# Two early weight loads on ScalarE's queue, one high part on VectorE, and the gate's small loads on SyncE's queue

## The chip, the cores and the metric

The kernel runs on one core of a Trainium2 chip. The metric is device time in microseconds (us); the time of a kernel is the median of its runs. The engines are named as in the profile: PE is TensorE (PEld its weight loads), DVE is VectorE, ACT is ScalarE, POOL is GpSimd, SP is SyncE. DMA issues can stand in the queue of SP, ACT or POOL.

## The reference

Two layers of an encoder trunk, in fp32, on x of 256 tokens by 2048 features. Each layer projects x once into many parts, runs three mixers side by side, multiplies each result by a SiLU gate, projects the concatenation back and normalizes:

```python
h = x @ w_in                                   # 2048 -> 6672 columns, cut into eleven parts
y_a = chunk_band_attention(a_q, a_k, a_v, rel_table)        # 8 heads of 128
log_g = log_sigmoid(b_lr @ gate_w + gate_b) / 16
y_b = rms(gla_chunk_recurrence(b_q, b_k, b_v, log_g)) * gla_norm_g   # 4 heads
mk, mv = split(mem @ w_mem_kv)                 # 256 memory tokens, 2048 -> 2 x 512
y_m = memory_attention(m_q, mk, mv)            # 4 heads of 128
y = concat([y_a * silu(a_z), y_b * silu(b_z), y_m * silu(m_z)])
x = layer_norm(alpha * x + y @ w_out)
```

## The kernel before

**Arithmetic.** PE multiplies in a rounded 32-bit form (fp32r). To keep fp32 accuracy each operand is split into a high part, the value rounded to fp32r, and a low part, the remainder. `parts` (L114) makes both: ACT casts the high part (L116), DVE subtracts it from the source for the low part (L117). A product is then three matmuls: high by high, low by high, high by low (`as_products`, L264, with x stationary and the weights moving; `ws_half`, L240, and `keys_of` with the weights stationary and the two parts of x side by side as the moving operand).

**Weights.** A piece of weights is two 128-row blocks of 512 columns (or four of 256, or two of 388). `piece` (L128) issues its load on SP into one of four `raw` buffers and splits it into one of four `wh` and one of four `wl` buffers. SP can issue a load once DVE has read the buffer's former contents, ACT can cast once PE is done with the former `wh`; so the loads, casts and subtractions run some pieces ahead of PE.

**Order.** PE's and SP's instructions keep the order in which the code writes them; DVE and ACT do so only inside the marked blocks, and elsewhere a scheduler places them. POOL's order is the scheduler's too. Waits between engines are semaphores. Behind the kernel's start the order is:

- six matmuls on a tile of zeros (L753), which PE runs as twelve passes, while the first data are on their way;
- `first_memory` (L191): the values and keys of the memory, in eight steps p of two 128-row blocks each. `first_pieces` (L153) issues and splits the loads of a step. In steps 0 and 1, for each of two blocks k: a 128 KB quarter of the memory's transpose (`x_part`, L163, into `early`, which lies in the tile `res`), the value weights (L177), the key weights (L179). The value weights of step 0, block 0 are cut in two halves of 256 columns, so that PE can start on the first half. All of these loads stand in SP's queue; DVE and ACT follow the written order here;
- `values_of` (L198) and `keys_of` (L205) are the products. In step 0, block 0 the values take twelve matmuls of 256 columns: the first half of the columns for both blocks of 128 tokens, then the second half;
- the query and key group of the gated linear attention (L783), then `gla_inputs` (L296): the gate matrix three times into `gwraw`, the gate bias `gb` and the norm's scale `ng`, five small loads on POOL's queue. ACT's copy at L305 and DVE's subtraction at L306 make the gate matrix's parts; they are used in `gla`, after the next group. In layer 0 the identity and a mask follow on SP (L789, L791);
- the value projections (L797), the attention heads, the gates, the output projection and the norm. In layer 1 the same without `first_memory`, and the norm at the end is split up by columns.

Of the kernel before, what the change touches and what calls it, by code (L numbers as in the profile page):

```python
# [8 lines left out]
F32 = mybir.dt.float32  # L9
# [4 lines left out]
ALU = mybir.AluOpType  # L14
# [4 lines left out]
P = 128  # L19
# [17 lines left out]
def hybrid_trunk_kernel(  # L37
# [7 lines left out]
    pe, dve, act, pool, sp = nc.tensor, nc.vector, nc.scalar, nc.gpsimd, nc.sync  # L45
# [42 lines left out]
    def nm(s):  # L88
        uid[0] += 1
        return f"{s}_{uid[0]}"  # L90

    def mm(o, l, r, start, stop):
        pe.matmul(o, l, r, start=start, stop=stop, skip_group_check=True)  # L93

    def bank():
        return psa.tile([P, 512], F32, name=nm("bk"), tag="bk")

    def scratch(shape, dtype=F32):
        return sc.tile(shape, dtype, name=nm("sc"), tag="sc")

    def small(shape, tag, bufs=1):
        return sm.tile(shape, F32, name=nm(tag), tag=tag, bufs=bufs)
# [6 lines left out]
    def operand():  # L109

        x = opp.tile([P, 4, 2, T], F32R, name=nm("x"), tag="x")
        return x[:, :, 0], x[:, :, 1], x.rearrange("p j h t -> p j (h t)")

    def parts(hi, lo, src):  # L114

        act.copy(hi, src)  # L116
        dve.tensor_tensor(lo, src, hi.bitcast(F32), op=ALU.subtract)  # L117
# [35 lines left out]
    def first_pieces(p, x):  # L153


        xsrc, j0 = memT[p // 2], p % 2 * 2
        xraw = early[:, p // 2]
        vsrc = w512[0, G_MV, p].rearrange("p (k n) -> p k n", k=2)
        ksrc = w512[0, G_MK, p // 2:8:4, :, j0 * 256:j0 * 256 + 512].rearrange("h p (k n) -> p k h n", k=2)
        raws, his, los = ([wp.tile([P, 2, 512], dt, name=nm(n), tag=n) for _ in range(2)]  # L160
                          for n, dt in (("raw", F32), ("wh", F32R), ("wl", F32R)))

        def x_part(j):  # L163
            sp.dma_start(xraw[:, j], xsrc[:, j])
            parts(x[0][:, j], x[1][:, j], xraw[:, j])

        def split(i, at):
            parts(his[i][at], los[i][at], raws[i][at])

        if p < 2:  # L170
            with tc.manual_schedule(engines={DVE, mybir.EngineType.Activation}):
                for k in range(2):
                    x_part(slice(j0 + k, j0 + k + 1))
                    cut = 2 if p == k == 0 else 1
                    for h in range(cut):
                        cs = slice(h * 512 // cut, (h + 1) * 512 // cut)
                        sp.dma_start(raws[0][:, k, cs], vsrc[:, k, cs])  # L177
                        split(0, (slice(None), k, cs))
                    sp.dma_start(raws[1][:, k].rearrange("p (h n) -> p h n", h=2), ksrc[:, k])  # L179
                    split(1, (slice(None), k))  # L180
        else:
            with tc.high_priority(AHEAD):
                x_part(slice(j0, j0 + 2))
                sp.dma_start(raws[0], vsrc)
                split(0, slice(None))
                for h in range(2):
                    sp.dma_start(raws[1][:, :, h * 256:(h + 1) * 256], ksrc[:, :, h])
                split(1, slice(None))
        return list(zip(his, los))

    def first_memory(mk, mv, each):  # L191

        memq = []
        accv = psd.tile([P, 2, 512], F32, name=nm("acc"), tag="acc")
        acck = psd.tile([P, 2, 2, T], F32, name=nm("acc"), tag="acc")
        blocks = [acck[:, b] for b in range(2)] + [bank().rearrange("p (h t) -> p h t", h=2) for _ in range(2)]

        def values_of(p, w, kk):  # L198

            for h in range(2 if p == kk == 0 else 1):  # L200
                cs = slice(h * 256, h * 256 + 256) if p == kk == 0 else slice(0, 512)
                for t in range(2):
                    as_products(accv[:, t, cs], t, memq, [x[:, :, cs] for x in w], p * 2 + kk, kk, -1 if h else 0)

        def keys_of(p, w, kk):  # L205
            (wh, wl), (xh, _, both), j = w, memq[p // 2], p % 2 * 2 + kk
            for b in range(4):
                mm(blocks[b].rearrange("p h t -> p (h t)"), wh[:, kk, b * P:(b + 1) * P], both[:, j], p == kk == 0, False)
            for b in range(4):
                mm(blocks[b][:, 1], wl[:, kk, b * P:(b + 1) * P], xh[:, j], False, p * 2 + kk == 15)  # L210

        late = None
        for p in range(8):
            if p % 2 == 0:
                memq.append(operand())
            v, k = first_pieces(p, memq[-1])
            for kk in range(2):
                values_of(p, v, kk)
                if p < 2:
                    keys_of(p, k, kk)  # L220
            if p == 6:
                late = k
            elif p > 1:
                if p == 7:
                    parts(*mv, accv)
                    for kk in range(2):
                        keys_of(6, late, kk)
                for kk in range(2):
                    keys_of(p, k, kk)
            each(p)  # L230
        for half in range(2):
            tmp = scratch([P, 2, T])
            if half == 0:
                total(tmp, acck[:, :, 0], acck[:, :, 1])
            else:
                for b in range(2):
                    total(tmp[:, b], blocks[2 + b][:, 0], blocks[2 + b][:, 1])
            parts(mk[0][:, half * 2:half * 2 + 2], mk[1][:, half * 2:half * 2 + 2], tmp)
# [21 lines left out]
    def total(dst, a, b, scale=1.0):  # L260
        act.mul(dst, b, scale)
        dve.scalar_tensor_tensor(dst, a, scale, dst, op0=ALU.mult, op1=ALU.add)  # L262

    def as_products(o, t, xq, w, kt, kk, first=0):  # L264
        wh, wl = w
        xh, xl, _ = xq[kt // 4]
        j, ts = kt % 4, slice(t * P, (t + 1) * P)
        mm(o, xh[:, j, ts], wh[:, kk], kt == first, False)
        mm(o, xl[:, j, ts], wh[:, kk], False, False)
        mm(o, xh[:, j, ts], wl[:, kk], False, kt == 15)  # L270
# [25 lines left out]
    def gla_inputs(l):  # L296

        gw = sm.tile([P, 256], F32R, name=nm("gw"), tag="gw")
        raw = hd.tile([48, 256], F32, name=nm("gwraw"), tag="pairs0")
        gb = small([P, 2], "gb")  # L300
        ng = small([P, 1], "ng")
        for i in range(3):
            pool.dma_start(raw[i * 16:i * 16 + 16], gate_w[l])
        pool.memset(gw.bitcast(F32), 0.0)
        tc.keep_in_program_order(act.copy(gw[:48], raw))  # L305
        tc.keep_in_program_order(dve.tensor_tensor(gw[32:48], raw[32:], gw[32:48].bitcast(F32), op=ALU.subtract))  # L306
        pool.dma_start(gb, gate_b[l])
        pool.dma_start(ng, norm_g[l])
        return gw, gb, ng

    def gla(gw, gb, ng, gq, gk, lr, asv, yraw):
# [438 lines left out]
    zeros = hd.tile([P, P], F32, name="zeros", tag="st")  # L750
    dve.memset(zeros, 0.0)
    idle = bank()
    for _ in range(6):  # L753
        mm(idle[:, :P], zeros, zeros, True, True)

    res = per.tile([P, 2, D], F32, name="res")
# [3 lines left out]
    for l in range(L):  # L760
# [3 lines left out]
        if l == 0:  # L764
            def each(p):
                if p in (2, 4, 6, 7):
                    xq.append(resident_quarter(len(xq), xT[len(xq)]))

            first_memory(mk, mv, each)
        else:  # L770
            memq = []
# [13 lines left out]
        if l > 0:  # L785
            waiting.append(gens[1])
        gp = gla_inputs(l)
        if l == 0:
            sp.dma_start(ident, ident_d)  # L789
# [11 lines left out]
        def heads(g):  # L801
            t = hd.tile([P, 4, T], F32, name=nm("qk"), tag="qk", bufs=4)
            for i, a, b in ws_group(w512[l, g], xq):
                total(t[:, i:i + 2], a, b)
            return t
# [25 lines left out]
        for half in range(2):  # L831
            values(2 + half)
            q = heads(G_AQ0 if half == 0 else G_AQ1)
            k = heads(G_AK0 if half == 0 else G_AK1)
# [36 lines left out]
        gb = []  # L871
        rows = norm_rows(l) if last else None
        for n in range(WO_N):
            if last:
                g, b = scratch([P, 512]), scratch([P, 512])
            else:
                both = per.tile([P, 2, 512], F32, name=nm("gb"), tag=f"yr{n}")
                g, b = both[:, 0], both[:, 1]
# [126 lines left out]
```

## Time and profile before

| | |
|---|---|
| median of 3 runs | 925.89 us (925.69 to 926.02) |
| profiled execution, its own time | 925.59 us |
| span of the profile | 923.8 us |
| mean DMA rate over the span | 194 GB/s |
| DMA rate in the first two of 40 slices | 306 and 334 GB/s |
| software DMA queue (POOL's) | 1920 packets, 4.36 MB |

The rows are read like this. In a table by stretches, each row gives a stretch in us from the span's start, its length, the busy time of each engine with its count of instructions, the granted clock, the mean busy share of the DMA engines and their rate. In a timeline, a row gives the start, the time from the first to the end of the last of the merged instructions, the engine, the line, the operation, what it writes and reads, its shape and count, and in brackets how long the engine sat idle before it and what released it. A q behind an engine's name marks its queue (issues of DMAs, semaphores). In a row of a group by line and shape, the busy time and the mean ns stand behind the bar. In a row of one line, three durations in ns (least, median, greatest) and the first and last start stand behind the count; in a row of DMA issues, the size and the us from issue to landing.

### The profile page before, as it was taken

What the parts mean: (1) busy time and instruction counts of PE and PEld (TensorE: products, weight loads), DVE (VectorE), ACT (ScalarE), POOL (GpSimd) and SP (SyncE); (2) the same over time, 40 slices, a digit from 0 to 9 for tenths busy, and PEclk for the clock granted to TensorE, in tenths of its full rate; (3) what the DMA queues carried; (4) which work ended last, traced back from release to release, by engine and by line L of the source; (5) the groups of instructions that cost most, each with busy time, mean ns of one, the idle gap of its engine ahead of it and who ended that gap; (6) DMA issues with size and microseconds to landing.
All of it is one profiled execution on the core that took longest, in us unless ns stands there. A gap on an engine that the chain in (4) does not pass through costs nothing.

```text
span 923.8 us, 14249 instructions
## 1 busy us (share of the span) xinstructions
PE 916.7 (99%) x5500; PEld 806.5 (87%) x5500; DVE 587.9 (64%) x812; ACT 498.2 (54%) x714; POOL 21.8 (2%) x49
## 2 busy tenths in 40 slices
PE   9999999999999999999999999999999999999997
PEld 7889998998888888888888899889888888888885
DVE  6764478665564666555587666975655555766566
ACT  6644485484454675433566445754744555754350
POOL 1000000000000000000000000000000000110000
PEclk9999999999999999999999999999999999999999
DMA  9955865546554566756675466546555544667652
GB/s 306 334 189 174 306 207 173 161 165 194 183 162 160 171 206 200 219 193 196 227 249 164 150 205 204 193 154 196 170 193 166 164 152 160 199 222 223 198 163 92
DMA packets 71253, 178.85 MB, mean 194 GB/s; under 512 B 7304, under 2 KB 31240, under 8 KB 70928
## 3 DMA queue, kind: packets, MB, share of 16 engines
q1 hardware_dynamic: 69120, 173.30, 57.1%
q0 software_dynamic: 1920, 4.36, 1.8%
q8 instruction: 43, 0.70, 0.3%
q10 hardware_dynamic: 144, 0.26, 0.1%
q14 instruction: 26, 0.21, 0.1%
HBM read 175.77 MB, written 2.10 MB: 193 GB/s over the span
## 4 chain that ended last, share of the span: by engine, by line
PE 98%; DMA 0%; DVE 0%; ACT 0%; SPq 0%; issue 0%
PE acc L93 89%; PE bk L93 8%; PE bk L526 1%; DMA raw<-w 0%; PE bk L561 0%; PE bk L590 0%; PE bk L494 0%; PE bk L393 0%; SPq L177 0%; ACT res L746 0%; ACT wh L116 0%; DVE stats L731 0%; PE bk L340 0%; DVE res L730 0%; DVE res L682 0%
## 5 line engine op out<-in xcount | busy, mean ns | idle before, releaser
L117 DVE TENSOR_TENSOR wl<-raw,wh 128x1024 fp32r<-128x1024 f32 (+3 forms) x321 | 370.0, 1154 | 255.9 <-ACT wh L116 254.9
L116 ACT CAST wh<-raw 128x1024 fp32r<-128x1024 f32 (+3 forms) x321 | 318.7, 994 | 329.9 <-PE acc L93 236.5
L93 PE MATMUL acc<-x,wh 128*128 128x512 f32 x1248 | 398.0, 400 | 0.1
L93 PE MATMUL acc<-wh,x 128*128 128x512 f32 (+2 forms) x1236 | 357.3, 370 | 0.1
L93 PEld LDWEIGHTS acc<-x,wl 128*128 128x128 f32 x1248 | 234.4, 188 | 55.3
L93 PEld LDWEIGHTS acc<-wh,x 128*128 128x128 f32 x1236 | 227.0, 188 | 27.9 <-ACT wh L116 0.6
L93 PE MATMUL acc<-x,wl 128*128 128x256 f32 x1248 | 246.0, 278 | 0.0
L93 PE MATMUL acc<-wl,x 128*128 128x512 f32 (+2 forms) x618 | 228.0, 369 | 0.0
L93 PEld LDWEIGHTS acc<-x,wh 128*128 128x128 f32 x1248 | 192.0, 189 | 1.9 <-ACT wh L116 0.4
L93 PEld LDWEIGHTS acc<-wl,x 128*128 128x128 f32 x618 | 116.0, 188 | 15.0 <-DVE wl L117 0.9
L518 ACT ACTIVATE sc<-sc,mx 128x128 f32<-128x128 f32 (+1 forms) x32 | 14.4, 450 | 20.3 <-DVE mx L516 20.3
L511 DVE SCALAR_TENSOR_TENSOR sc<-bk,bias 128x384 f32<-128x384 f32 x16 | 8.9, 554 | 12.7 <-PE bk L93 12.7
L382 ACT ACTIVATE sc<-sc 128x512 f32<-128x512 f32 x12 | 7.6, 633 | 12.5 <-DVE sc L380 12.5
L117 DVE TENSOR_TENSOR x<-sc,x 128x512 fp32r<-128x512 f32 x20 | 13.3, 684 | 0.7 <-ACT x L116 0.7
L116 ACT CAST x<-raw 128x1024 fp32r<-128x1024 f32 x5 | 5.3, 1053 | 15.3 <-DMA raw<-memT 12.7
L117 DVE TENSOR_TENSOR x<-res,x 128x512 fp32r<-128x512 f32 (+2 forms) x14 | 10.5, 765 | 4.2 <-ACT x L116 4.1
L93 PE MATMUL bk<-qk,qk 128*128 128x128 f32 (+1 forms) x64 | 13.1, 326 | 0.0
L117 DVE TENSOR_TENSOR x<-raw,x 128x1024 fp32r<-128x1024 f32 x5 | 6.1, 1225 | 10.9 <-ACT x L116 10.9
L93 PE MATMUL bk<-sc,asv 128*128 128x256 f32 (+1 forms) x64 | 13.0, 326 | 0.0
L262 DVE SCALAR_TENSOR_TENSOR sc<-acc,sc 128x512 f32<-128x512 f32 x19 | 12.9, 681 | 0.0
L116 ACT CAST x<-sc 128x512 fp32r<-128x512 f32 x20 | 11.8, 615 | 1.3 <-DVE sc L598 1.3
L623 DVE SCALAR_TENSOR_TENSOR res<-res,acc 128x512 f32<-128x512 f32 x15 | 9.7, 684 | 4.2 <-PE acc L93 4.2
(209 smaller groups left out, 567.8 us busy)
## 6 DMA issues: line engine op xcount, KB each, us to landing
raw<-w SPq DMA_DIRECT2D x214, 512.0 KB, 3.9
raw<-w SPq DMA_DIRECT2D x64, 388.0 KB, 3.3
raw<-w SPq DMA_DIRECT2D x83, 256.0 KB, 3.2
bias<-relw SPq DMA_DIRECT2D x16, 192.0 KB, 4.1
res<-xT SPq DMA_DIRECT2D x4, 512.0 KB, 5.0
res<-xn SPq DMA_DIRECT2D x1, 2048.0 KB, 8.2
raw<-memT SPq DMA_DIRECT2D x4, 512.0 KB, 4.3
res<-memT SPq DMA_DIRECT2D x6, 256.0 KB, 6.1
```

Of the source, the lines that this page charges most:

```text
L93: pe.matmul(o, l, r, start=start, stop=stop, skip_group_check=True)
L116: act.copy(hi, src)
L117: dve.tensor_tensor(lo, src, hi.bitcast(F32), op=ALU.subtract)
L262: dve.scalar_tensor_tensor(dst, a, scale, dst, op0=ALU.mult, op1=ALU.add)
L382: act.activation(dd, dd, AF.Abs)
L511: dve.scalar_tensor_tensor(s, pb[:, :384], SCALE, bias[h], op0=ALU.mult, op1=ALU.add)
L518: act.activation(s[:, own[t]], s[:, own[t]], AF.Exp, bias=mx[:, t:t + 1], accum_out=zs[:, t:t + 1])
L526: pe.transpose(pt[:, i * P:(i + 1) * P], s[:, i * P:(i + 1) * P], ident)
L623: dve.scalar_tensor_tensor(r, r, ALPHA, acc, op0=ALU.mult, op1=ALU.add)
```

## The change

Five edits. The two halves of the first value weights are issued on ACT's queue, ahead of everything else that ACT does; SP no longer issues them. For the first quarter of x, DVE makes the high part as a copy instead of ACT's cast. In step 0, block 0 the products are written in another order: for each half of the columns, each of the three operand pairs is taken for both blocks of tokens before the next pair. The five small loads of the gate go into SP's queue, at the place where `gla_inputs` is called, in both layers. And one of the six matmuls on zeros is left out.

```diff
         def x_part(j):
             sp.dma_start(xraw[:, j], xsrc[:, j])
-            parts(x[0][:, j], x[1][:, j], xraw[:, j])
+            if p == j.start == 0:
+                dve.tensor_copy(x[0][:, j], xraw[:, j])
+                dve.tensor_tensor(x[1][:, j], xraw[:, j], x[0][:, j].bitcast(F32), op=ALU.subtract)
+            else:
+                parts(x[0][:, j], x[1][:, j], xraw[:, j])
...
             with tc.manual_schedule(engines={DVE, mybir.EngineType.Activation}):
+                cuts = {}
+                for k in range(2):
+                    n = 2 if p == k == 0 else 1
+                    cuts[k] = [(slice(None), k, slice(h * 512 // n, (h + 1) * 512 // n)) for h in range(n)]
+                    if n == 2:
+                        for at in cuts[k]:
+                            act.dma_start(raws[0][at], vsrc[at])
                 for k in range(2):
                     x_part(slice(j0 + k, j0 + k + 1))
-                    cut = 2 if p == k == 0 else 1
-                    for h in range(cut):
-                        cs = slice(h * 512 // cut, (h + 1) * 512 // cut)
-                        sp.dma_start(raws[0][:, k, cs], vsrc[:, k, cs])
-                        split(0, (slice(None), k, cs))
+                    for at in cuts[k]:
+                        if len(cuts[k]) == 1:
+                            sp.dma_start(raws[0][at], vsrc[at])
+                        split(0, at)
                     sp.dma_start(raws[1][:, k].rearrange("p (h n) -> p h n", h=2), ksrc[:, k])
                     split(1, (slice(None), k))
...
-            for h in range(2 if p == kk == 0 else 1):
-                cs = slice(h * 256, h * 256 + 256) if p == kk == 0 else slice(0, 512)
-                for t in range(2):
-                    as_products(accv[:, t, cs], t, memq, [x[:, :, cs] for x in w], p * 2 + kk, kk, -1 if h else 0)
+            if p == kk == 0:
+                (wh, wl), (xh, xl, _) = w, memq[0]
+                for cs in (slice(0, 256), slice(256, 512)):
+                    for i, (a, b) in enumerate(((xh, wh), (xl, wh), (xh, wl))):
+                        for t in range(2):
+                            mm(accv[:, t, cs], a[:, 0, t * P:(t + 1) * P], b[:, 0, cs], i == cs.start == 0, False)
+                return
+            for t in range(2):
+                as_products(accv[:, t], t, memq, w, p * 2 + kk, kk)
...
         for i in range(3):
-            pool.dma_start(raw[i * 16:i * 16 + 16], gate_w[l])
+            sp.dma_start(raw[i * 16:i * 16 + 16], gate_w[l])
...
-        pool.dma_start(gb, gate_b[l])
-        pool.dma_start(ng, norm_g[l])
+        sp.dma_start(gb, gate_b[l])
+        sp.dma_start(ng, norm_g[l])
...
-    for _ in range(6):
+    for _ in range(5):
         mm(idle[:, :P], zeros, zeros, True, True)
```

## The prediction

> **What bounds the kernel now.** I read the page's busy line and the summary of the chain of waits first, then a table of busy time by stretches, cut where the first memory products begin (4.10), where the first key products begin (6.65), after the last early wait (17.55) and before the closing normalization (902).
>
> ```profile
> PE 916.7 (99%) x5500; PEld 806.5 (87%) x5500; DVE 587.9 (64%) x812; ACT 498.2 (54%) x714; POOL 21.8 (2%) x49
> ...
> PE 98%; DMA 0%; DVE 0%; ACT 0%; SPq 0%; issue 0%
> ```
>
> ```profile
> 4.10:6.65 2.55, 2.40 (x13) 1.86 (x13) 0.85 (x3) 1.08 (x3) 0.45 (x2) 1.00 0.99 319
> 6.65:10.90 4.25, 4.25 (x23) 3.67 (x24) 3.10 (x6) 2.52 (x5) 0.00 (x0) 1.00 0.91 266
> 10.90:17.55 6.65, 6.63 (x34) 5.11 (x33) 4.82 (x8) 4.92 (x8) 0.00 (x0) 1.00 1.05 390
> 17.55:902.00 884.45, 884.45 (x5350) 781.32 (x5349) 564.73 (x761) 485.41 (x692) 18.33 (x38) 1.00 0.60 194
> ```
>
> The columns are the stretch, its length, then busy time of PE, PEld, DVE, ACT and POOL, the granted clock, the DMA share and GB/s. From 17.55 to 902.00 PE is busy for all of 884.45 us. Nothing that makes DVE, ACT, POOL or SP quicker in there moves the end; what the change can win lies ahead of 17.55, and what it can lose lies wherever it makes PE wait. So the ramp has to be read row by row, by engine.
>
> ```profile
> 0.74 0.38 SPq L164 DMA_DIRECT2D res<-memT  x1
> 1.18 0.89 SPq L177 DMA_DIRECT2D raw<-w  x2
> 2.11 0.43 SPq L179 DMA_DIRECT2D raw<-w  x1
> ```
>
> ```profile
> 0.73 1.28 ACT L116 ACT_TABLE_LOAD   x1 [0.73 <-PEq L995]
> 3.22 0.40 ACT L116 CAST x<-res 128x256 fp32r<-128x256 f32 x1 [1.20 <-DMA res<-memT]
> 3.64 0.40 ACT L116 CAST wh<-raw 128x256 fp32r<-128x256 f32 x1
> 4.84 0.41 ACT L116 CAST wh<-raw 128x256 fp32r<-128x256 f32 x1 [0.80 <-DMA raw<-w]
> 5.97 0.62 ACT L116 CAST wh<-raw 128x512 fp32r<-128x512 f32 x1 [0.73 <-DMA raw<-w]
> ```
>
> ```profile
> 1.05 2.93 PE L93 MATMUL bk<-zeros 128*128 128x128 f32 x12 [1.05 <-DVE eps L759]
> 4.10 0.74 PE L93 MATMUL acc<-wh,x 128*128 128x256 f32 x2
> 4.67 0.29 PE L93 MATMUL acc<-wl,x 128*128 128x256 f32 x1
> 4.80 0.41 PE L93 MATMUL acc<-wh,x 128*128 128x256 f32 x2
> 5.05 0.28 PE L93 MATMUL acc<-wl,x 128*128 128x256 f32 x1
> 5.30 0.50 PE L93 MATMUL acc<-wh,x 128*128 128x256 f32 x2
> ...
> 6.65 0.73 PE L93 MATMUL acc<-x,wh 128*128 128x512 f32 x2
> ```
>
> Read down: SP issues x, the two halves of the first value weights, then the first key weights, one after another. ACT makes x's high part (3.22), the first half's high part (3.64), and PE starts at 4.10, when the latter is done (3.64 + 0.40 = 4.04). Then ACT waits for weights twice, 0.80 and 0.73 us. PE needs 2.55 us (4.10 to 6.65) for the twelve 256-column products of step 0; three of them take 0.38 (4.67 to 5.05), 0.127 each, so twelve would need 1.52 and 1.03 us go in waits and in the slow first pair. The key products at 6.65 begin when their cast ends: 5.97 + 0.62 = 6.59.
>
> **The change part by part.**
>
> *First weights from ACT's queue.* SP loses the two issues at 1.18 and everything behind them moves up by 2.11 - 1.18 = 0.93 us; the key weights are then issued at 1.18. If their landing keeps its distance from the issue (5.97 - 2.11 = 3.86), ACT casts them at 5.04 to 5.66 and the key products can start at 5.72: 0.93 us earlier. This holds only if PE has finished its twelve products by then. ACT issues the halves from 0.73. What one issue costs ACT the trace shows once, at the end of the kernel; SP's above are 0.38 to 0.45, and POOL's, for other loads, 1.63 / 3 = 0.54:
>
> ```profile
> L705 ACTq DMA_DIRECT2D out<-res x1: 371/371/371, 919.4 to 919.4; - x1
> ```
>
> ```profile
> 1.27 1.63 POOL L303 DMA_DIRECT2D gwraw<-gate_w  x3 [0.82 <-POOLq L995]
> ```
>
> Two of 0.37 to 0.54, then the table load of 1.28, which stands behind them in the changed program: ACT is ready at 2.75 to 3.10, ahead of the first landing at 3.22, so the two issues cost ACT nothing. I take 0.45 each, as on SP. The first half is then issued beside x instead of 0.44 behind it, the second near 1.18 instead of 1.62, 0.44 sooner: its cast can start at 4.4 instead of 4.84.
>
> *x's high part on DVE.* Not in the trace in this form. The nearest rows are two DVE casts, and ACT's own cast of 0.40:
>
> ```profile
> L342 DVE CAST lrT<-bk 128x256 fp32r<-128x256 f32 x2 | 0.8, 424 | 1.3 <-PE bk L340 1.3
> ...
> L792 DVE CAST lmask<-lm 128x384 uint8<-128x384 int32 x1 | 0.4, 355 | 0.0
> ```
>
> So 0.36 to 0.42 us; I take 0.42, the row with the same shape. DVE had nothing to do there. ACT casts the first half beside it: both end near 3.22 + 0.42 = 3.64, at worst 0.2 later if the landings of x and the half share the transfer engines. First real matmul at 3.7 instead of 4.10. The next pair needs x's low part (DVE, another 0.42: 4.06), the third pair the low weights (4.48). With the first two pairs still at the slow pace of 4.10 to 4.67 (0.57 for two) the first half ends near 4.9. The second half is cast from 4.4, so its six products run at 0.127 each and end near 5.65. The key products then start at 5.72, set by their weights as before. One zeros product fewer: the zeros' twelve passes take 2.93 us, ten end at about 3.5, ahead of 3.7; with twelve, PE would be held to 3.98. The new order of the products (both token blocks before the next operand) is the same count of the same size: nothing beyond what is said.
>
> *Behind 5.7.* Two waits of the weight loader are left in the ramp:
>
> ```profile
> 11.34 0.19 PEld L93 LDWEIGHTS acc<-wl,x 128*128 128x128 f32 x1 [0.25 <-DVE wl L117]
> ...
> 17.20 0.19 PEld L93 LDWEIGHTS acc<-wl,x 128*128 128x128 f32 x1 [0.46 <-DVE wl L117]
> ```
>
> Both are waits on data that come down the same SP queue, now 0.93 earlier. PE is 0.93 earlier too, so I expect them to stay about as they are. After 17.2 the weights run ahead of PE. The first piece behind it:
>
> ```profile
> 20.63 1.23 DVE L117 TENSOR_TENSOR wl<-raw,wh 128x1024 fp32r<-128x1024 f32 x1 [0.19 <-ACT wh L116]
> ```
>
> ```profile
> 22.89 0.40 PE L93 MATMUL acc<-wl,x 128*128 128x512 f32 x1
> ```
>
> Ready at 21.86 and used at 22.89: 1.03 us in hand, enough even if only PE moved. So what is won at 5.7 reaches the end.
>
> *Gate loads on SP.* Five issues per layer leave POOL, where they ran at 1.27 to 4.2 in layer 0, and come behind the eighth weight load of the gla query/key group.
>
> ```profile
> 52.21 0.33 SPq L141 DMA_DIRECT2D raw<-w  x1
> 52.59 0.43 SPq L789 DMA_DIRECT2D ident<-ident  x1
> ```
>
> ```profile
> 56.76 0.23 DVE L793 TENSOR_TENSOR eye<-ident 128x64 f32<-128x64 f32 x1 [0.34 <-DMA ident<-ident]
> ```
>
> ```profile
> 507.24 0.33 SPq L141 DMA_DIRECT2D raw<-w  x1
> ```
>
> ```profile
> 510.49 0.33 SPq L141 DMA_DIRECT2D raw<-w  x1
> ```
>
> ```profile
> L305 ACT CAST gw<-gwraw x2: 392/392/393, 73.6 to 528.9; 48x256 fp32r<-48x256 f32 x2
> ```
>
> Five at 0.43 are 2.15 us of SP. In layer 1 SP sits idle from 507.57 to 510.49 between two weight loads, 2.9 us. In layer 0 they stand ahead of the identity load: it is issued near 54.7 and DVE's eye, which waited 0.34 for it at 56.76, runs near 59; one low-part subtraction is behind it on DVE. The gate weights are first read at 73.6 and 528.9, 20 us after the issue. Cost 0; without that cover up to 2.15 a layer. Taking them out of the ramp may speed its transfers. That is worth between nothing and the waits that are then still left (the second rival: 2.1 - 0.93, about 1.2); I take 0.1, near the lower end, because no row shows who slows whom.
>
> *Order elsewhere.* In the changed program ACT and DVE run in the same order but for one place, two heads of layer 1 near 650 to 665, where the gla norm and the softmax of two heads change turns. The tightest pair there:
>
> ```profile
> 663.87 0.55 DVE L521 TENSOR_SCALAR sc<-sc,zs 128x128 f32<-128x128 f32 x2
> ```
>
> ```profile
> 665.59 0.49 PE L526 MATMUL bk<-ident,sc 128*128 128x128 f32 x3
> ```
>
> The second head's weights were ready at 664.42, 1.17 us early. No step that changes turns is longer than a 128x1024 subtraction (1.23, at 20.63 above). One such step more ahead of the second head uses up the 1.17, two would cost 1.3. I take one: cost 0, upper end 1.3.
>
> **Sum.** 0.93 from the queue slots and 0.1 from the lighter ramp, 0 lost in layer 1: -1.03. The profiled execution took 925.59 (span 923.8 and 1.8 around it), so 924.56; it lies 0.30 below the median of the runs shown, 925.89, so on that footing **924.9**.
>
> **The rivals.**
>
> *Transfers hold the ramp.* From 10.90 to 17.55 the DMA share is 1.05: if the transfers, not the issues, set the landings there, then the data of 17.20 come no sooner, PE arrives early and waits. Gain 0 to 0.5, say -0.2: 925.7. Against it: 266 GB/s in 6.65 to 10.90 beside 390 later, so there was room. The Trainium skill ("DMA: Bandwidth & Descriptors", section "Issuing engines are not separate DMA queues") says that transfers started by different engines run on the same 16 DMA engines, so that only issue time is saved; issue time is the 0.93 above, and where the share is full it argues for this rival.
>
> *More than the slots.* With the small gate loads out of the ramp, all its waits go: 0.4 at the start, 1.03 up to 6.65, up to 0.25 + 0.46 behind: at most 2.1. Taking three quarters, -1.6: 924.3.
>
> *The clock stays low longer (slower).* The first pair took 0.57, later ones 0.25; full pace shows at 4.67, 3.62 us after the zeros began, while the granted clock reads 1.00 throughout. Real work now starts 0.4 sooner and one zeros product is gone. Should PE's pause before the first real product (some 0.2 by my sum, 0.12 before) make it count as not busy, the slow pace would last another 3.62 us: 1.8 lost, some 0.3 of it in waits, +1.5 - 1.03: 926.4. It decides from the pause at which the gate lets go, which no row shows; 0.12 is below it. The Trainium skill ("TensorE: Matmul & The Clock Gate", part 1) says that the clock opens after a busy window of about 3.4 us, which runs freely and does not start with the kernel, so that the opening moves by some 0.5 us between runs; by it, as an estimate, half of that, 0.25 us of time, either way. The three runs, within 0.33 us, speak against a large scatter.
>
> *SP blocks (slower).* If the five small loads hold the weight loads behind them until they land, 2.15 of issue plus 4.2:
>
> ```profile
> ng<-norm_g POOLq DMA_DIRECT2D x1, 0.5 KB, 4.2
> ```
>
> that is 6.4 against 2.9 idle: 3.5 a layer eats into weights that run ahead of PE. It decides when it passes that lead; with half of it lost in each layer, +3.5 - 1.03: 928.4. No later load in the trace waits so for an earlier one.
>
> That the change does not do what it says (the halves land later from ACT's queue than from SP's) would leave the key weights first in line and the start at 4.1: still about -0.5, inside the range.
>
> **How the numbers follow.** Forecast 0.56, transfers 0.20, more than the slots 0.15, clock 0.05, SP 0.04. The range 924.0 to 926.2 holds the first three. A measurement of this kernel tells 0.2%, 1.85 us, from no change: faster by that (below 924.04) 0.04, from the second rival's far end; slower (above 927.74) 0.05, from SP and a bad case of the clock; within it 0.91.
>
> **What would show it.** ACT's first rows are two DMA issues from 0.73, the table load behind them; SP's second row is the key weights at 1.18. The first real matmul is at 3.6 to 3.8, the first key product at 5.7, the weight loader's last wait near 16.3; from there to the closing stage PE is busy without a break, the same 884 us. SP's five issues near 51.7 and 506.7 leave no PE wait behind them. It is wrong if the key product starts before 5.3 or after 6.1, if the wait near 16.3 has grown by what the start won, or if PE waits near 60, 520 or 665.

## The result, and the profile after

| | before | changed |
|---|---|---|
| median of 22 runs each | 925.92 us (925.35 to 926.39) | 927.15 us (925.98 to 928.83) |
| profiled execution, span | 925.59, 923.8 | 927.14, 925.4 |
| time against before | | 1.0012 [1.0006, 1.0017] |

The changed kernel is slower by 1.23 us, 0.13%: below the 0.2% that the prediction set as a difference, yet with an interval clear of 1. The forecast was 924.9, the top of the range 926.2.

The page's busy line and the summary of its chain of waits say that PE is the bound, as before:

```profile
PE 917.6 (99%) x5498; PEld 808.1 (87%) x5498; DVE 587.6 (63%) x813; ACT 497.2 (54%) x713; POOL 16.7 (2%) x39
...
PE 99%; DMA 0%; DVE 0%; ACT 0%; issue 0%
```

They hide the loss, since PE is busy while it is slow. The table by stretches, cut where the memory products (4.16) and the key products (7.17) begin and after the last of the former waits:

```profile
4.16:7.17 3.01, 3.01 (x13) 2.81 (x14) 1.85 (x6) 1.82 (x5) 0.00 (x0) 1.00 1.04 366
7.17:10.90 3.73, 3.73 (x14) 3.17 (x14) 3.65 (x8) 3.32 (x7) 0.00 (x0) 1.00 1.07 363
10.90:17.55 6.65, 6.65 (x35) 5.62 (x34) 5.21 (x6) 4.75 (x7) 0.00 (x0) 1.00 1.03 386
17.55:903.00 885.45, 885.45 (x5357) 782.25 (x5356) 562.27 (x760) 483.44 (x690) 15.93 (x33) 1.00 0.60 193
```

PE is busy for the whole of each stretch and the granted clock reads 1.00. But the twelve products ahead of the key products took 2.55 us before and take 3.01 now. (The stretch counts 13 matmuls, one that only touches its edge among them.) The reason shows only in a timeline of PE, where the pace can be read off the starts:

```profile
1.05 2.50 PE L93 MATMUL bk<-zeros 128*128 128x128 f32 x10 [1.05 <-DVE eps L774]
4.16 1.22 PE L93 MATMUL acc<-wh,x 128*128 128x256 f32 x4 [0.61 <-ACT wh L116]
5.18 0.63 PE L93 MATMUL acc<-wl,x 128*128 128x256 f32 x2
...
8.02 1.05 PE L93 MATMUL bk<-x,wh 128*128 128x512 f32 x2
...
9.30 0.63 PE L93 MATMUL bk<-x,wl 128*128 128x256 f32 x2
9.72 0.73 PE L93 MATMUL acc<-wh,x 128*128 128x512 f32 x2
10.29 0.39 PE L93 MATMUL acc<-wl,x 128*128 128x512 f32 x1
10.52 0.62 PE L93 MATMUL acc<-wh,x 128*128 128x512 f32 x2
```

The zeros end at 3.55, the first product waits 0.61 for the first half's high part, and then a pair of 512 columns takes 1.05 until about 10, and 0.62 from there. In the profile of before the full pace was there at 4.67. Here it comes at 10.05 (the start of the second matmul of the pair at 9.72). In this document the full pace is dated by the start of the first matmul that runs at it.

What the weight loader waits for in the first 25 us, first before, then changed (total, times, longest):

```profile
PEld acc L93 <- ACT wh L116: 0.9, 3, 0.4
PEld acc L93 <- DVE wl L117: 0.9, 3, 0.5
```

```profile
PEld acc L93 <- ACT wh L116: 1.1, 2, 0.9
```

So the data waits behind the first product are gone, but for 0.2. They did not become time won: PE is slow enough that it meets no wait.

The queues of SP and ACT, and what ACT and DVE did with the first data:

```profile
0.74 0.38 SPq L164 DMA_DIRECT2D res<-memT  x1
1.17 0.42 SPq L189 DMA_DIRECT2D raw<-w  x1
```

```profile
0.73 0.89 ACTq L182 DMA_DIRECT2D raw<-w  x2
1.65 1.28 ACT L116 ACT_TABLE_LOAD   x1 [1.65 <-PEq L1010]
3.71 0.40 ACT L116 CAST wh<-raw 128x256 fp32r<-128x256 f32 x1 [0.77 <-DMA raw<-w]
5.26 0.92 ACT L116 CAST wh<-raw 128x256 fp32r<-128x256 f32 x2 [1.15 <-DMA raw<-w]
```

```profile
3.54 0.29 DVE L166 CAST x<-res 128x256 fp32r<-128x256 f32 x1 [2.52 <-DMA res<-memT]
```

The issues stand where they were forecast; the data do not. x, issued at 0.74 in both kernels, is used at 3.54 instead of 3.22, the first half at 3.71 instead of 3.64, and the second half at 5.26 instead of 4.84, although it was issued sooner. (The last ACT row merges two casts; the second, of the key weights, ends at 6.18.) The DMA queues from 1.5 to 3.5 us, while these data travel, first before, then changed (packets, MB, share of the 16 engines):

```profile
q1 hardware_dynamic: 398, 0.37, 65.8%
q0 software_dynamic: 36, 0.02, 3.6%
```

```profile
q1 hardware_dynamic: 250, 0.24, 41.2%
q10 hardware_dynamic: 178, 0.17, 29.1%
```

SP's loads are in q1, ACT's in q10, POOL's in q0. All queues together move 194 GB/s before and 203 changed, almost the same. But SP's queue, which carries x, moved 0.24 MB for 0.37 in this time, while ACT's moved 0.17.

One more part of the loss lies at the other end. ACT's last issue, an output, stood at 919.41 before, 4.4 us ahead of the span's end; now 4.72 us ahead of it. In the changed kernel the DMA queues of the span from 915 on have an instruction load, which before has not:

```profile
920.65 0.36 ACTq L720 DMA_DIRECT2D out<-res  x1
```

```profile
q14 instruction: 1, 0.01, 0.3%
```

Matched matmul by matmul, the changed kernel lags by 1.70 us at 10, by 1.22 at 20, by 1.24 at the last matmul, and by 1.55 at the end. From 20 to the last matmul the lag stays between 1.22 and 1.26.

### The profile page after: what moved, and what is told of

Its sections match the earlier page's. It is cut to its first block, busy times and chain, and to the rows that moved or that the text cites. A ratio compares the mean times of both kernels' runs of the same rounds, so it can differ in the third digit from the quotient of the medians.

```text
span 925.4 us, 14233 instructions
## 1 busy us (share of the span) xinstructions
PE 917.6 (99%) x5498; PEld 808.1 (87%) x5498; DVE 587.6 (63%) x813; ACT 497.2 (54%) x713; POOL 16.7 (2%) x39
## 4 chain that ended last, share of the span: by engine, by line
PE 99%; DMA 0%; DVE 0%; ACT 0%; issue 0%
PE acc L93 89%; PE bk L93 8%; PE bk L541 1%; PE bk L576 0%; PE bk L605 0%; DMA raw<-w 0%; PE bk L509 0%; PE bk L408 0%; ACT res L761 0%; DVE stats L746 0%; PE bk L355 0%; DVE res L745 0%; ACT wh L116 0%; DVE res L697 0%; DVE mvt L700 0%
## 5 line engine op out<-in xcount | busy, mean ns | idle before, releaser
L117 DVE TENSOR_TENSOR x<-raw,x 128x1024 fp32r<-128x1024 f32 x5 | 6.1, 1225 | 10.1 <-ACT x L116 10.0
L93 PEld LDWEIGHTS bk<-sc,asv 128*128 128x128 f32 x64 | 11.3, 189 | 1.2
```

## The experiments

**Theory (the clock).** PE's slow pace ends some us after PE began to work without a break. A long pause between the zeros and the first product starts this anew. **Rivals:** the second half's late landing holds PE; the small loads on SP or the order in layer 1 cost the time; the loads on ACT's queue are bad by themselves.

All runs, 11 of each kernel, in order. The ratio is to the kernel before on the same chip. Pause (from the zeros' end), first product and full pace are from the one profiled execution, worked out from the matmuls' starts; "–" is no pause. The medians of the kernel before, measured beside these, were 925.95 to 926.10. Of the ratios' intervals only those of e10 and e18 leave out 1, so one row against before says little. What follows rests on kernels set against each other: every run of e5, at most 925.85, lies below every run of e9, at least 926.09 (on two chips, where before had 926.10 and 926.01).

| run | median us (range) | ratio | pause | first product | full pace | profiled |
|---|---|---|---|---|---|---|
| e1 changed, 6 zeros | 925.79 (925.20–927.36) | 1.0002 [0.9993, 1.0010] | 0.12 | 4.10 | 6.1 | 925.91 |
| e2 before, 5 zeros | 925.94 (925.44–926.35) | 1.0000 [0.9991, 1.0009] | 0.29 | 3.86 | 7.9 | 925.91 |
| e3 before, halves on ACT | 925.31 (925.10–927.05) | 0.9996 [0.9988, 1.0005] | 0.28 | 4.27 | 6.5 | 925.34 |
| e4 before, gate on SP | 925.78 (924.99–926.46) | 0.9998 [0.9989, 1.0007] | – | 3.99 | 7.1 | 925.77 |
| e5 changed, 8 zeros | 925.44 (925.12–925.85) | 0.9993 [0.9984, 1.0002] | – | 4.49 | 5.3 | 925.37 |
| e6 before, 4 zeros | 926.35 (925.68–926.76) | 1.0002 [0.9993, 1.0010] | 0.84 | 3.97 | 7.1 | 925.68 |
| e7 changed, halves on SP | 926.02 (925.60–926.54) | 1.0000 [0.9991, 1.0008] | 0.39 | 3.94 | 5.8 | 925.83 |
| e8 the same, 7 zeros | 926.37 (925.39–927.17) | 1.0004 [0.9995, 1.0013] | – | 4.06 | 5.7 | 926.37 |
| e9 changed again | 926.88 (926.09–927.46) | 1.0007 [0.9998, 1.0016] | 0.73 | 4.29 | 10.2 | 927.25 |
| e10 changed, filler | 927.05 (926.55–927.48) | 1.0010 [1.0001, 1.0018] | 0.80 | 4.36 | 8.4 | 926.55 |
| e11 second half on SP | 926.86 (926.02–927.53) | 1.0007 [0.9998, 1.0016] | 1.04 | 4.59 | 9.2 | 926.89 |
| e12 the same, 8 zeros | 925.73 (925.18–926.10) | 0.9995 [0.9986, 1.0004] | – | 4.52 | 7.0 | 925.79 |
| e13 changed, 3 zeros | 926.83 (926.33–927.76) | 1.0008 [0.9999, 1.0017] | 1.89 | 4.59 | 10.7 | 927.53 |
| e14 before, 2 zeros | 926.29 (925.55–926.75) | 1.0002 [0.9993, 1.0010] | 1.66 | 3.93 | 10.1 | 926.71 |
| e15 changed, 10 zeros | 925.50 (925.30–926.01) | 0.9995 [0.9986, 1.0004] | – | 5.35 | 5.7 | 925.71 |
| e16 before, halves on ACT, 8 zeros | 925.52 (925.23–925.73) | 0.9992 [0.9983, 1.0001] | – | 4.70 | 5.4 | 925.39 |
| e17 changed, 8 zeros, gate on POOL | 925.42 (924.94–925.62) | 0.9993 [0.9984, 1.0002] | – | 4.35 | 4.6 | 924.94 |
| e18 changed, 8 zeros, gate split | 925.01 (924.67–925.46) | 0.9990 [0.9981, 0.9999] | – | 4.49 | 5.7 | 924.73 |

### One part of the change at a time

**e1**, the changed kernel with the sixth product on zeros back:

```diff
-    for _ in range(5):
+    for _ in range(6):
```

> The changed kernel with the sixth matmul on zeros put back. Theory (the clock opens late because PE pauses 0.61 us, from 3.55 to 4.16, before the first product): the zeros end near 3.98, the pause falls to about 0.2, full pace shows near 4.7 instead of 10.0, and the time falls by about 2 us below the changed kernel, to 925.0 to 925.4 (before: 925.9). Rival (the later landings of x, 3.54 against 3.22, and of the second half, 5.26 against 4.84, cost the time): full pace as late as before, 927.1.

Seven of its runs lie at 925.2 to 925.9, four at 926.7 to 927.4. One product on zeros, 0.43 us of cover, moves most runs from one group to the other; with the pause near 0.12 it seems to stand at the edge. The forecast of 925.0 to 925.4 missed: the median is 925.79, and the full pace came at 6.1 instead of 4.7.

**e2**, the kernel before with one zeros product fewer:

```diff
-    for _ in range(6):
+    for _ in range(5):
```

> The kernel before with five matmuls on zeros instead of six, nothing else. Theory of the clock: the zeros end near 3.55, the first product still starts at 4.10, the pause is 0.55, full pace comes some 3 to 5 us later than 4.67, time 927.0 to 927.6. Rival of the landings: nothing changes, 925.9.

No loss, against the forecast of the theory. It had put the first product at 4.10; but x was cast at 2.89 and the product ran at 3.86, after a pause of 0.29 and not 0.55. The full pace did come late, at 7.9.

**e3**, the kernel before with the first edit alone:

```diff
+                    if n == 2:
+                        for at in cuts[k]:
+                            act.dma_start(raws[0][at], vsrc[at])
```

> The kernel before with only the two first weight halves issued by ACT (x's high part stays on ACT, six zeros, old order of the products, gate loads on POOL). Theory of the clock: with six zeros the pause stays under 0.3 and the time is 925.0 to 925.9. Rival of the landings: x and the second half land 0.3 to 0.4 later, the start slips, 926.2 or more.

Ten of eleven runs lie at 925.1 to 925.6, one at 927.05. The ten lie below the 925.97 that before had beside it, so this edit seems to gain something in most runs; the interval of the ratio still holds 1. Its first data, by ACT's timeline:

```profile
3.50 0.41 ACT L116 CAST x<-res 128x256 fp32r<-128x256 f32 x1 [0.57 <-DMA res<-memT]
3.81 0.40 ACT L116 CAST wh<-raw 128x256 fp32r<-128x256 f32 x1
5.39 0.93 ACT L116 CAST wh<-raw 128x256 fp32r<-128x256 f32 x2 [1.18 <-DMA raw<-w]
```

x comes later than in e2 (2.89) with nothing else changed ahead of it, and the second half at 5.39.

**e4**, the kernel before with the gate's small loads on SP:

```diff
-            pool.dma_start(raw[i * 16:i * 16 + 16], gate_w[l])
+            sp.dma_start(raw[i * 16:i * 16 + 16], gate_w[l])
...
-        pool.dma_start(gb, gate_b[l])
-        pool.dma_start(ng, norm_g[l])
+        sp.dma_start(gb, gate_b[l])
+        sp.dma_start(ng, norm_g[l])
```

> The kernel before with only the gate's five small loads on SP's queue. Clock theory: pause as before, no small loads in the ramp, so the second half lands sooner than 4.84: 925.2 to 925.9. A rival in which the small loads on SP hold the weights: 926.5 or more with PE waits near 60 or 520.

The rival "SP blocks" falls: from 20 us to the closing normalization PE waits for nothing. The key weights are cast at 5.19 instead of 5.97 in this one profile. That the small loads held them up is not shown: e7 and e8, without these loads in the ramp, have 5.69 and 5.66, and e6 and e14, with them, 5.74 and 5.70. The close is 0.30 longer than before (5.85 from the last matmul's start to the span's end, for 5.55).

### More and fewer zeros

In the expectations of e13, e14 and e15, S is the start of the first product and O the start of the full pace. Between the two PE runs at about half pace (0.43 us for 512 columns instead of 0.23) and so loses about (O − S)/2; the end then moves as S + (O − S)/2, which is (S + O)/2.

**e5** and **e15**, the changed kernel with eight and with ten:

```diff
-    for _ in range(5):
+    for _ in range(8):
```

> The changed kernel with eight matmuls on zeros. They end near 4.45, behind the landing of x and the first half, so PE does not pause before the first product. Theory (a pause ahead of the first product delays the clock): no run late, all within 925.2 to 926.0, where six zeros still gave 4 of 11 runs at 926.7 to 927.4. Rival (the landings cost the time): the first product is 0.3 later than with six, 926.2 or more.

```diff
-    for _ in range(5):
+    for _ in range(10):
```

> The changed kernel with ten zeros: they hold PE to about 5.3, O stays between 4.5 and 7.9. Form with (S + O)/2: S is 0.8 later than with eight, but of that only what PE's wait for the second half (0.31) does not take: 925.5 to 926.0, 0.1 to 0.5 above the eight zeros (925.44). Rival (more zeros are always better): below 925.4.

PE's timeline in e5:

```profile
1.06 3.78 PE L93 MATMUL bk<-zeros 128*128 128x128 f32 x16 [1.06 <-DVE eps L774]
4.49 1.05 PE L93 MATMUL acc<-wh,x 128*128 128x256 f32 x4
5.37 0.40 PE L93 MATMUL acc<-wl,x 128*128 128x256 f32 x2
```

The first product starts 0.33 later than in the changed kernel and the end comes 1.4 us earlier (against e9; 1.7 against the first median), because there is no pause and the pace is full at 5.3. Ten zeros, which hold PE to 5.35, are as good as eight.

**e13**, the changed kernel with three:

```diff
-    for _ in range(5):
+    for _ in range(3):
```

> The changed kernel with three zeros: they end near 2.7, the first product is at 4.2 to 4.3 as with five, the wait 1.5 instead of 0.6 to 0.7. Form with (S + O)/2: S and the range of O (7.6 to 11) are as with five zeros, so the median is 926.8 to 927.4, no later. Rival (the cost grows with the wait or with each missing zero): 928 or more.

A pause of 1.89 costs no more than one of 0.7: the loss is a step, not a slope.

**e6** and **e14**, the kernel before with four and with two:

```diff
-    for _ in range(6):
+    for _ in range(4):
```

> The kernel before with four matmuls on zeros: they end near 3.1, the first product at 3.9 to 4.1, a pause of 0.7 to 1.0 with no other change; five zeros left 0.29 and cost nothing. Theory of the pause: the clock opens at 8 to 11 and the time is 926.8 to 927.5, as in the changed kernel. Rival (the pause does not matter, it is the changed loads): 925.9.

```diff
-    for _ in range(6):
+    for _ in range(2):
```

> The kernel before with two zeros: they end near 2.3, first product at 3.9 to 4.0, wait 1.6. Form with (S + O)/2: O between 7.4 and 10.8, end between 925.7 and 927.4, median 926.2 to 926.8, near the 926.35 of four zeros. Rival (grows with the wait): 927.5 or more.

Their pauses are as long as the changed kernel's, and in e14 the full pace is as late (10.1); yet they lose only about 0.2, where the theory had forecast 0.9 or more for e6. (The profiled run of e6, with the full pace at 7.1, was the fastest of its eleven, 925.68, and may not stand for the others.) Two things pay for it. The first product comes at 3.93 to 3.97, and the data waits that before has are gone in e14 and down to two, 0.6 in all, in e6. PEld's only wait in e14 between 3 and 25 us:

```profile
3.93 0.50 PEld L93 LDWEIGHTS acc<-wh,x 128*128 128x128 f32 x2 [1.95 <-ACT wh L116]
```

Slow pace hides waits, and waits hide slow pace: the later of the two sets the time.

The form of the expectations bears this out. In the profiles of the changed kernel, e9, e11 to e15 and e18, which meet hardly any data waits, (S + O)/2 runs from 5.1 to 7.6, and the start of the last matmul less (S + O)/2 is always 912.3 to 912.6. In before, which meets waits, it is 913.9.

### Where the halves are issued

**e7** and **e8**, the changed kernel with the halves back on SP, and the same with seven zeros:

```diff
-                    if n == 2:
-                        for at in cuts[k]:
-                            act.dma_start(raws[0][at], vsrc[at])
...
-                        if len(cuts[k]) == 1:
-                            sp.dma_start(raws[0][at], vsrc[at])
+                        sp.dma_start(raws[0][at], vsrc[at])
```

> The changed kernel with the two first halves issued by SP again, behind x (x's high part on DVE, gate loads on SP, new order of the products and five zeros stay). Theory: alone in the queue x lands at 2.9 to 3.2 instead of 3.54, the first product is at 3.6 to 3.9, the pause 0.1 to 0.35, the clock opens as before: 925.0 to 925.8. Rival (the loads on ACT were a gain and something else costs 1.2): 927.1 or more.

> As e7 with seven matmuls on zeros, ending near 4.0: no pause at all in any run, first product at 4.0 to 4.1. Theory: 925.0 to 925.7 and a narrow scatter; better than the kernel before by 0.2 to 0.8, since nothing but x and the weights is in the ramp. Rival: as e7.

e7 undoes the loss, though its 926.02 lies a little above its forecast: x comes at 3.18, the product at 3.94. e8 missed its forecast: without the issue on ACT, cover for the clock wins nothing, since data waits of 0.43, 0.20, 0.20, 0.43 and 0.47 stand between 8.5 and 17.7. So the gain of the changed kernel with a covered pause (e5) hangs on the first edit, as e3 and e16 say too, and in the changed kernel the pause takes it.

**e9**, the changed kernel once more, beside **e10**, with a product on zeros put between the two halves of the columns:

```diff
                 for cs in (slice(0, 256), slice(256, 512)):
+                    if cs.start:
+                        mm(idle[:, :P], zeros, zeros, True, True)
```

> The changed kernel itself once more, beside its variants on one chip, since five zeros with the loads on SP (e7) and even four zeros in the kernel before (e6) were not late. If its lateness belongs to the kernel: median 926.8 to 927.4. If it belonged to the chip of the first comparison: 925.4 to 926.

> The changed kernel with one more matmul on zeros between the two column halves of the first block; five zeros ahead as in the change. It fills PE's second wait (0.28 us for the second half, 5.44 to 5.72) and leaves the first (0.61, 3.55 to 4.16). Theory, second form (both waits together keep PE's busy share too low in the stretch that decides the clock): only the first wait is left, as long as or shorter than the 0.84 of e6, so the median is 925.6 to 926.4. Theory, first form (the wait ahead of the first product alone): no better than the changed kernel, 926.8 to 927.4. Rival of the landings: no better either.

The changed kernel is again late. Filling the second wait (0.2 at 5.7) does not help, so it is not what keeps the pace low. That part of the theory fell; the first pause is left.

**e11** and **e12**, the changed kernel with only the first half on ACT, and the same with eight zeros:

```diff
-                        for at in cuts[k]:
-                            act.dma_start(raws[0][at], vsrc[at])
+                        act.dma_start(raws[0][cuts[k][0]], vsrc[cuts[k][0]])
...
-                        if len(cuts[k]) == 1:
+                        if at != cuts[0][0] or p > 0:
```

> The changed kernel with the second half issued by SP behind x, only the first half by ACT; five zeros. If the second half lands late in the change because it shares the transfer engines from a second queue with the key weights and the next x (5.26 to 5.42 in all four kernels that issue it on ACT, 3.9 to 4.8 from SP), it lands at 4.0 to 4.6 here and PE's second wait goes: 925.4 to 926.2. If it is late for another reason, it stays at 5.2 or more and the time at 926.8 or more.

> e11 with eight zeros: neither wait is left. Theory: narrow scatter, 925.0 to 925.6, at or below e5 (925.44) and 0.4 to 0.9 below the kernel before; a candidate for the best version. Rival of the landings: as e11.

ACT in e11:

```profile
0.74 0.41 ACTq L181 DMA_DIRECT2D raw<-w  x1
4.14 0.71 ACT L116 CAST wh<-raw 128x256 fp32r<-128x256 f32 x2 [1.68 <-DMA raw<-w]
5.35 0.62 ACT L116 CAST wh<-raw 128x512 fp32r<-128x512 f32 x1 [0.50 <-DMA raw<-w]
```

The second half is there at 4.5 and the key weights sooner, as wanted, and the time is no better: e11's forecast missed. The first half and x are late (4.14 and 3.96, as in e13, which has both halves on ACT), and the pause is 1.04. This rules out the rival "second half". With the pause covered (e12) 1.1 us come back; e12's 925.73 is still above its forecast of 925.0 to 925.6, so the second half on SP wins nothing.

**e16**, the kernel before with the halves on ACT, as in e3, and eight zeros:

```diff
-    for _ in range(6):
+    for _ in range(8):
```

> The kernel before with only the two halves on ACT, and eight zeros in place of six. If the loads on ACT are the whole gain of the change and the zeros its whole loss: 925.1 to 925.6, no run above 926.2, as e5. If x's high part on DVE, the order of the products or the gate loads on SP carry part of e5's gain: 925.6 to 926.0.

It needs neither DVE's copy nor the new order of the products nor the small loads on SP to be as good as e5. Its close is 0.26 shorter (5.57 for 5.83), and its last matmul starts 0.25 later in the profile, so a small gain of these edits in the ramp is not ruled out.

### The end of the span

**e17** and **e18**, the changed kernel with eight zeros, and the gate loads all on POOL, or layer 0's on SP and layer 1's on POOL:

```diff
-            sp.dma_start(raw[i * 16:i * 16 + 16], gate_w[l])
+            pool.dma_start(raw[i * 16:i * 16 + 16], gate_w[l])
...
-        sp.dma_start(gb, gate_b[l])
-        sp.dma_start(ng, norm_g[l])
+        pool.dma_start(gb, gate_b[l])
+        pool.dma_start(ng, norm_g[l])
```

```diff
-            sp.dma_start(raw[i * 16:i * 16 + 16], gate_w[l])
+            (sp if l == 0 else pool).dma_start(raw[i * 16:i * 16 + 16], gate_w[l])
...
-        sp.dma_start(gb, gate_b[l])
-        sp.dma_start(ng, norm_g[l])
+        (sp if l == 0 else pool).dma_start(gb, gate_b[l])
+        (sp if l == 0 else pool).dma_start(ng, norm_g[l])
```

> The changed kernel with eight products on zeros and the five small gate loads of each layer back on POOL's queue. In the traces so far the time from the last matmul to the end of the span is 5.55 to 5.57 us wherever the gate loads are on POOL (the kernel before, and with two, four or five zeros, with its weights on ACT) and 5.80 to 5.85 wherever they are on SP (the changed kernel in all forms, and the kernel before with this edit alone), and one instruction fetch lies in the last microseconds only in the latter. Theory 'the gate loads' place costs 0.3 at the end': the tail is again 5.55 and the time is 925.44 - 0.28 = 925.15 (924.9 to 925.4). Rival 'POOL's small loads slow the ramp': the tail is 5.55 as well, but the key weights are cast 0.2 to 0.5 later than the 5.73 of the changed kernel with eight zeros, and what is won at the end is lost there: 925.4 to 925.7.

> The changed kernel with eight products on zeros; the gate loads of layer 0 on SP, those of layer 1 on POOL. If the 0.3 us at the end hang on how long POOL's stream of instructions is (five of the ten issues are gone from it, not ten), the tail is either 5.55 or 5.83 and nothing between, with an instruction fetch in the last microseconds in the second case only: 925.15 or 925.44. If they hang on SP's longer queue, half of the loads would give a tail between, near 5.7: 925.3. Rival 'POOL's small loads slow the ramp': layer 0's are out of the ramp here, so that the ramp is as in the changed kernel with eight zeros, and quicker than with all the gate loads on POOL.

From the last matmul's start to the span's end: 5.83 in e5, 5.55 in e17 as expected, and 5.24 in e18, which neither theory had. ACT's last issue in e18, whose span is 922.9:

```profile
918.84 0.35 ACTq L720 DMA_DIRECT2D out<-res  x1
```

That is 4.1 us ahead of the end, for 4.4 before and 4.72 changed. The trace's last instructions say what differs. SP's closing waits on semaphores follow each other at 0.06 us: from the last landing on there are eight in e17, six in e5 and three in e18. And in e5 POOL stands still for 0.43 behind its last clearing step, where e17 and e18 have 0.09; only e5 has the instruction load there. So e18 has the shortest list and no stop. Measured side by side, e18 is 0.41 below e17, of which the close explains 0.31. e17's time missed by 0.27, and its key weights were no later than e5's (both behind the second half's cast), so what POOL's loads cost in its ramp stays open. e18 is the fastest kernel of this study, 0.94 us below before.

## Why the prediction was wrong, point by point

**First weights from ACT's queue.** Right on the issues: SP's second row is the key weights at 1.17, ACT's two issues take 0.89, and the table load behind them hides. Wrong in "the first half is then issued beside x instead of 0.44 behind it, the second near 1.18 instead of 1.62 … its cast can start at 4.4". Issued sooner is not landed sooner: with two queues at work the second half was cast at 5.25 to 5.57 wherever both halves were on ACT, against 3.9 to 4.8 with all on SP, and x at 3.4 to 4.0 against 2.9 to 3.2. The key products were not held by their weights (ready at 6.18) but by PE, busy until 7.17, so the 0.93 of the sum was not won. The Trainium skill's section that the prediction named ("DMA: Bandwidth & Descriptors", "Issuing engines are not separate DMA queues") has it that such transfers share the same engines; the trace agrees: from 1.5 to 3.5 us the rate was 203 GB/s for 194, shared by two queues, and x was used 0.3 later.

**x's high part on DVE.** The copy took 0.29 for 0.42, as a price harmless. The step that failed stands here: "first real matmul at 3.7 instead of 4.10" and so a pause of "some 0.2". The product came at 4.16. With the zeros ending at 3.55, as forecast, the pause is 0.61. It was bounded "at worst 0.2 later if the landings … share the transfer engines"; it was 0.46 later, and the price of that was not 0.46 but a step.

**The clock rival happened.** Named with 0.05 and 926.4, "it decides from the pause at which the gate lets go". The mechanism was right and mis-sized: the slow pace was to last another 3.62, and between the profiled executions the full pace moved by 5.38, from 4.67 to 10.05. At half pace half of that is lost: 2.7 us, an estimate from these two times. The 1.22 seen at 20 us leaves about 1.5 that came back. Of these 1.2 are waits on data that PE no longer met: PEld's waits behind the first product fell from 1.4 to 0.2. The forecast also let the won slots (0.93) and the clock's loss (1.5) stand side by side; they are rivals for the same microseconds, since PE can't use sooner data while it is slow. e5, e12, e13 and e15 show it by experiment: cover the pause and the loss goes, lengthen it and it does not grow.

**Behind 5.7.** The waits at 11.34 and 17.20 did not stay: PE, later than its data, met neither. That the lead behind 20 us is enough was right. The rival "transfers hold the ramp" expected its cost at 17.20; shared transfers did cost time, but ahead of the first product.

**Gate loads on SP.** Five issues at 53.8 and at 508.9 without a wait of PE: right. "Cost 0" was wrong by 0.30 at the very end, for which the prediction had no term, and nothing of the 0.1 for "taking them out of the ramp" is seen at the end of the changed kernel.

**Order elsewhere.** Right: the lag is the same 1.26 us at 630 and at 790.

**Sum.** In the profiled executions +1.22 in the ramp, +0.02 on the way, +0.30 in the close: +1.55, against −1.03.

What stays open: at which pause the clock's count starts anew. In the profiles the pauses up to 0.4 left the full pace at 4.6 to 7.9, and those from 0.6 on put it at 8.4 to 10.7. But e6 had 7.1 after 0.84. The 7.9 of e2, after 0.29, lies 4.1 us behind its first product, so it fits either count. And e1 has four late runs, with 0.12 in the one that was profiled. Each kernel was profiled once, so a pause that scatters from run to run can't be told from a threshold that isn't sharp. Nor do the times of e2 and e7 settle it, since in e14 a full pace at 10.1 cost only 0.2. In most runs fewer zeros and a longer pause come together, so whether the pause itself counts, or how long PE was busy ahead of it, is open too. That x lands late because ACT's transfers share its rate fits the bytes of the two queues, and e7, where x is back at 3.18; the single transfers were not followed.

## What to carry to other kernels

Where PE is kept warm by dummy work, size that work by the latest first product, with some to spare: too much cost nothing here (ten zeros, 925.50), one product too little 1.1 us (e9 against e1). An idle engine's queue brings issue time, and takes landing time from its neighbours. Here that paid some 0.6 us where the dummy work covered the later landing (e5, e16), and cost time where it did not (e9). With the halves on SP and no pause (e8) nothing was won. In a ramp, take the waits on data and the slow clock as two bounds of which the later counts, never as a sum.

## What the runs showed of the hardware

- Full pace comes 3.5 to 6.9 us after PE began to work without a break: counted from the zeros' start at 1.05 in the thirteen profiles with no pause or a short one (e17 at 4.6, e2 at 7.9), and 3.1 to 6.2 us behind the first product in the seven whose pause was over 0.6 (e6, e14). The Trainium skill ("TensorE: Matmul & The Clock Gate", part 1) puts the opening after a busy window of 3.4 us that runs freely. As an estimate from that page, one whole window is done 3.4 to 6.8 us after the start; the thirteen agree to 0.1. The 3.1 of e6 is shorter than one such window, so its pause seems not to have started the count anew. The traces don't agree with the page's scatter of 0.5 us: 3 us here, over thirteen kernels profiled once each. At half pace this scatter is worth some 1.5 us of time, as an estimate; the 33 runs of before beside e9 spread over 1.8 (925.27 to 927.03).
- The granted clock says nothing of it. The page of the changed kernel has it at nine tenths or more in every slice, and the stretches above read 1.00 where a pair of 512 columns took 1.05 instead of 0.62:

```profile
PEclk9999999999999999999999999999999999999999
```

- The last microseconds of this program depend on where ten small loads are issued: 5.24 to 5.85 us from the last matmul's start to the end.
